# Feed-forward input of an encoder trunk: ten of 22 gate/up tile pairs by seven block products, low parts on VectorE, two kept operands in DRAM

## The chip, the cores and the metric

The kernel runs on one core of one Trainium2 chip. The time is that of one launch on the device in microseconds, the median of several runs. Durations come from the hardware profile of one more execution. Engines are named as the profile names them: PE is TensorE's matmul, PEld its weight load, DVE VectorE, ACT ScalarE, POOL GpSimd, SP the queue that issues every DMA here. L and a number is a line of the kernel before; lines of the changed kernel are said to be its.

## What is computed

Two layers; each is a feed-forward, a token mixer, and a feed-forward, with a layer norm behind each. The change touches only the four feed-forwards (x is 512 x 1024, w_in 1024 x 5632, w_out 2816 x 1024, all float32):

```python
def swiglu(x, w_in, w_out):
    gate, up = jnp.split(x @ w_in, 2, axis=-1)
    return (jax.nn.silu(gate) * up) @ w_out
...
x = layer_norm(DN_ALPHA * x + 0.5 * swiglu(x, ffn_w_in[i, 0], ffn_w_out[i, 0]), ln_g[i, 0], ln_b[i, 0])
```

## The kernel before

Every float32 operand is held as a high part (a rounded copy, made by ScalarE) and a low part (what is left, by a subtraction): this is `split`, L276 for the high and L277 for the low part. A product is three matmuls: high by high, high by low, low by high (`mm3`, L286 to L288).

**The input half.** The hidden width of 2816 is 22 tiles of 128 channels. For each tile f the kernel loads two weight tiles of 512 KB, the gate's and the up's (`load_unit`, L245, into `raw`, two buffers; split into `w`, three buffers), and makes one projection each: 8 chunks of the 1024 input channels by 3 matmuls, 128 x 512 outputs, into a PSUM bank. A tile's two weights are called a pair below. ScalarE takes the SiLU of the gate (L491), VectorE multiplies by the up projection (L493) into `ar`.

**The output half** is a product of 2 x 2 blocks done with seven block products instead of eight. For it the loop over c (11 steps, two tiles f = 2c and 2c + 1 each, called a round below) prepares two things: `sums` loads 1 MB of w_out into `ra` (one buffer), makes four combinations (L894 to L897), writes two of them to the DRAM buffer `d_late` and splits three into `wx` (three buffers); and the rest of the loop combines `ar` (L498 to L501) and splits it: three parts into `an` (one buffer), four into `keep`, which stays in SBUF for the whole feed-forward. `early` (L923) multiplies `an` by the three `wx` for the step before; it stands behind the first tile's projections. Behind the loop four more products (V, Y, Z, Y) use the four kept parts, with weights loaded from w_out and `d_late`.

Combinations and splits of weights run on GpSimd; those of `ar` are shared between VectorE and GpSimd.

**What sets the order.** The program is written engine by engine; a scheduler orders each engine's instructions by its own timeline of the program. Each engine then works strictly in that order, and waits for what its next instruction needs. A tile's buffer is given again when the last reader of its former content is done; a load waits for that on SP.

**Where a feed-forward starts.** In all but the first, half of the first two pairs (tokens 0 to 255) is multiplied while the norm before still works; `follow` does the other half. The new `xT`, x transposed with its high and low part, is complete only then.

## Time and profile before

| | us |
|---|---|
| median of 3 runs | 2185.05 |
| lowest and highest | 2183.64, 2185.83 |
| the profiled execution | 2179.1 |
| its span | 2177.3 |
| first feed-forward, its loop | about 19 to 294 |
| granted TensorE clock, mean | 0.996 |

The span is the time from the first to the last instruction in the profile; the execution's own time is 1.8 us more. In a row of the profile's groups stand line, engine, operation, what it writes and reads, shapes, count, then busy us, mean ns of one, and idle time ahead of it with what ended it. A row that begins with two times is of a timeline: start and length. A row with three numbers between slashes gives the least, the median and the most ns of one. A row that begins with a window gives the busy us of PE, PEld, DVE, ACT and POOL with counts, the granted clock, the DMA engines' share and GB/s (or PE alone).

In the first loop a round takes 25.84 us: 114 matmuls of width 512 (96 for the two pairs, 18 for the early products), one behind the other.

### The profile page before, as it was taken

What the parts mean: (1) busy time and instruction counts of PE and PEld (TensorE: products, weight loads), DVE (VectorE), ACT (ScalarE), POOL (GpSimd) and SP (SyncE); (2) the same over time, 40 slices, a digit from 0 to 9 for tenths busy, and PEclk for the clock granted to TensorE, in tenths of its full rate; (3) what the DMA queues carried; (4) which work ended last, traced back from release to release, by engine and by line L of the source; (5) the groups of instructions that cost most, each with busy time, mean ns of one, the idle gap of its engine ahead of it and who ended that gap; (6) DMA issues with size and microseconds to landing.
All of it is one profiled execution on the core that took longest, in us unless ns stands there. A gap on an engine that the chain in (4) does not pass through costs nothing.

```text
span 2177.3 us, 35335 instructions
## 1 busy us (share of the span) xinstructions
PE 2138.7 (98%) x13952; PEld 1686.0 (77%) x13952; DVE 1052.1 (48%) x1526; ACT 954.7 (44%) x1675; POOL 1392.8 (64%) x1226
## 2 busy tenths in 40 slices
PE   9999999999999999999999999999999999999998
PEld 8888888888888888888888877446666568888876
DVE  3223355377333333553333569636888554333345
ACT  3333345377333333453333444537777434333333
POOL 5988855555478778578888543046767614877753
PEclk9999999999999999999999999999999999999999
DMA  6444462332244444544444553853444552444443
GB/s 210 150 155 144 142 230 97 116 114 76 91 162 140 141 145 136 212 141 142 144 137 144 198 175 125 288 172 104 133 122 128 165 190 83 150 135 141 140 165 126
DMA packets 145366, 321.47 MB, mean 148 GB/s; under 512 B 31056, under 2 KB 51152, under 8 KB 145200
## 3 DMA queue, kind: packets, MB, share of 16 engines
q1 hardware_dynamic: 145200, 319.21, 45.0%
q8 instruction: 110, 1.80, 0.3%
q14 instruction: 56, 0.46, 0.1%
HBM read 261.22 MB, written 45.88 MB: 141 GB/s over the span
## 4 chain that ended last, share of the span: by engine, by line
PE 91%; DMA 3%; DVE 2%; ACT 1%; issue 1%; POOL 1%; SPq 0%; DVEq 0%; ACTq 0%; POOLq 0%
PE bank L287 17%; PE bank L286 17%; PE bank L288 17%; PE bank L923 17%; PE a L1115 5%; PE bank L349 4%; PE g L1439 1%; PE y L1115 1%; DMA wv<-in_w_rv_dram 1%; PE bank L1306 1%; PE m L1115 1%; PE bank L677 1%; PE y L1614 1%; PE c L1607 1%; PE y L1637 1%
## 5 line engine op out<-in xcount | busy, mean ns | idle before, releaser
L277 POOL TENSOR_TENSOR w<-raw,w 128x1024 fp32r<-128x1024 f32 x198 | 485.7, 2455 | 224.4 <-ACT w L276 216.9
L286 PE MATMUL bank<-xT,w 128*128 128x512 f32 x1264 | 493.4, 390 | 0.0
L287 PE MATMUL bank<-xT,w 128*128 128x512 f32 x1264 | 492.3, 389 | 0.0
L288 PE MATMUL bank<-xT,w 128*128 128x512 f32 x1264 | 491.9, 389 | 0.0
L276 ACT ACTIVATE w<-raw 128x1024 fp32r<-128x1024 f32 x202 | 213.0, 1058 | 312.9 <-POOL ts L894 123.1
L493 DVE SCALAR_TENSOR_TENSOR ar<-bank,tmp 128x512 f32<-128x512 f32 x88 | 60.9, 692 | 570.3 <-PE bank L288 560.2
L288 PEld LDWEIGHTS bank<-xT,w 128*128 128x128 f32 x1264 | 237.3, 188 | 49.9
L286 PEld LDWEIGHTS bank<-xT,w 128*128 128x128 f32 x1264 | 237.3, 188 | 48.6
L287 PEld LDWEIGHTS bank<-xT,w 128*128 128x128 f32 x1264 | 237.4, 188 | 48.2
L923 PE MATMUL bank<-wx,an 128*128 128x512 f32 x792 | 187.5, 389 | 0.0
L923 PEld LDWEIGHTS bank<-wx,an 128*128 128x128 f32 x792 | 148.7, 188 | 31.2
L923 PE MATMUL bank<-w,ring 128*128 128x512 f32 x720 | 168.8, 390 | 1.9 <-POOL w L277 1.7
L277 POOL TENSOR_TENSOR wx<-ra,wx 128x512 fp32r<-128x512 f32 x132 | 167.0, 1291 | 3.1 <-ACT wx L276 3.1
L277 DVE TENSOR_TENSOR ring<-ar,ring 128x1024 fp32r<-128x1024 f32 x44 | 122.5, 2785 | 87.7 <-ACT ring L276 87.6
L923 PEld LDWEIGHTS bank<-w,ring 128*128 128x128 f32 x720 | 134.9, 188 | 31.1 <-POOL w L277 2.7
L491 ACT ACTIVATE tmp<-bank 128x512 f32<-128x512 f32 x88 | 52.6, 597 | 233.4 <-PE bank L288 233.2
L1546 POOL TENSOR_TENSOR tm<-qs,zs 128x126 f32<-128x126 f32 (+22 forms) x248 | 103.6, 418 | 79.3 <-issue 35.8
L1548 POOL TENSOR_TENSOR zs<-zs,tm 128x126 f32<-128x126 f32 (+22 forms) x248 | 110.9, 447 | 19.4
L276 ACT ACTIVATE wx<-ra 128x512 fp32r<-128x512 f32 x132 | 82.7, 632 | 79.3 <-PE bank L923 66.3
L277 POOL TENSOR_TENSOR ring<-raw,ring 128x1024 fp32r<-128x1024 f32 x24 | 60.1, 2515 | 78.8 <-ACT ring L276 78.8
L277 POOL TENSOR_TENSOR w<-xT,w 128x1024 fp32r<-128x1024 f32 x25 | 62.7, 2511 | 45.2 <-ACT w L276 45.2
L499 DVE TENSOR_TENSOR ar<-ar 128x256 f32<-128x256 f32 x44 | 90.3, 2052 | 1.5
(346 smaller groups left out, 3946.3 us busy)
## 6 DMA issues: line engine op xcount, KB each, us to landing
raw<-in_ffn_w_in_dram SPq DMA_DIRECT2D x176, 512.0 KB, 3.5
ra<-in_ffn_w_out_dram SPq DMA_DIRECT2D x44, 1024.0 KB, 4.9
xT<-d_late SPq DMA_DIRECT2D x29, 512.0 KB, 5.0
xT<-in_ffn_w_out_dram SPq DMA_DIRECT2D x23, 512.0 KB, 4.6
d_late<-ts SPq DMA_DIRECT2D x44, 256.0 KB, 3.0
d_late<-ra SPq DMA_DIRECT2D x44, 256.0 KB, 2.0
raw<-in_w_qkv_dram SPq DMA_DIRECT2D x16, 512.0 KB, 3.6
raw<-in_ffn_w_out_dram SPq DMA_DIRECT2D x12, 512.0 KB, 3.6
```

What stands on the lines that cost most here:

```text
L276: self.hi = self.nc.scalar.activation(h, raw, AF.Copy).ins
L277: self.lo = (eng or self.nc.vector).tensor_tensor(l, raw, h.bitcast(F32), ALU.subtract).ins
L286: nc.tensor.matmul(out, wh, xh, start=start, stop=False)
L287: nc.tensor.matmul(out, wh, xl, start=False, stop=False)
L288: nc.tensor.matmul(out, wl, xh, start=False, stop=stop)
L349: nc.tensor.matmul(acc[t, h], a, u[:, i, h * 512 : (h + 1) * 512], start=first and n == 0, stop=last and n == 2)
L493: nc.vector.scalar_tensor_tensor(raw[:, 3:7:3] if j else raw[:, 0:8:7], halves_of(pu), 0.5, halves_of(s), ALU.mult, ALU.mult)
L499: nc.vector.tensor_tensor(a(2), a(1), a(0), ALU.subtract)
L923: self.nc.tensor.matmul(acc, lhs, u[:, i], start=bool(first) and m == 0, stop=last and m == 2, skip_group_check=more)
L1115: self.nc.tensor.matmul(out[hs], w[:, hs], x, start=start, stop=stop)
L1546: nc.gpsimd.tensor_tensor(tv, qs[:, s, 0:s].rearrange("p (a o) -> p a o", o=1).broadcast_to([P, s, n]), zs[:, s : s + 1, c0:].broadcast_to ...
L1548: nc.gpsimd.tensor_tensor(zs[:, 0:s, c0:], zs[:, 0:s, c0:], tv, ALU.add)
```

## The change

Ten of the 22 pairs, the odd f from 3 on, are no longer computed by the plain projection. x (tokens by channels) and the pair's weights are taken as 2 x 2 blocks: input channels in two halves, tokens in two halves, gate and up as the two columns. The new class `Seven` makes seven products of blocks, each 4 chunks by 3 matmuls of 128 x 256. For it,

- `mixes` makes four combinations of the blocks of x once per feed-forward on VectorE, with splits (`right`, four ring buffers), in the two rows `gbc` and `bbc` that later hold the norm's parameters;
- `operands` loads the pair's two raw tiles and makes, in place, combinations of the weight blocks: two go to `w` (`ua`, `ub`), one to `one` and two to `pair`, single buffers in two rings;
- `products` makes the seven products in two banks. Partial results are copied from bank to bank and to `tmp` by ScalarE (the changed kernel's L971), added by VectorE (L996, L998), and gated (L1000, L1002). All pairs from f = 2 on use the same two banks.

The rings that this takes held half of `keep`: two of the four kept parts are now split into `away`, written to the DRAM buffer `d_away` each round, and read back by `recall` into freed rings for the last two products. The low parts and the combinations of `sums`, of the loop and of its weights go to VectorE; the norm's parameters are loaded behind the loop.

```diff
+SEVEN = range(3, NF, 2)
...
+        seven = Seven(self, xT, w_in)
         with self.pool("fa") as pool:
             out.pool = pool
-            keep = [self.ring().rearrange("p (i n s) -> p i n s", i=2, n=4) for _ in range(npairs)]
+            keep = [self.ring().rearrange("p (c n i s) -> p c n i s", c=2, n=2, i=2) for _ in range(npairs // 2)]
+            keep = [k[:, c] for k in keep for c in range(2)] + [seven.rest.rearrange("p (n i s) -> p n i s", n=2, i=2)]
             for c in range(npairs):
-                if c == 2 and not params:
-                    with self.behind(self.asked):
-                        params = self.ln_params(ln)
                 with self.behind(*() if c or ln else (self.asked,)):
                     out.sums(c)
                 raw = pool.tile([P, 8, 256], F32, name="ar", tag="ar", bufs=1)
                 for j in range(2):
                     f = 2 * c + j
+                    dst = raw[:, 3:7:3] if j else raw[:, 0:8:7]
                     if f == 0:
                         pps = self.follow()
+                    elif f in SEVEN:
+                        seven.products(f, dst)
                     elif not pps:
-                        us = self.units if f == 1 else [self.load_cols(w_in, FF * i + f * P) for i in range(2)]
-                        pps = [self.proj_cols(u, xT) for u in us]
-                    pg, pu = pps.pop(0), pps.pop(0)
-                    s = self.tmp()
-                    nc.scalar.activation(s, pg, AF.Silu)
-
-                    nc.vector.scalar_tensor_tensor(raw[:, 3:7:3] if j else raw[:, 0:8:7], halves_of(pu), 0.5, halves_of(s),
-                                                   ALU.mult, ALU.mult)
+                        us = self.units if f == 1 else [self.load_cols(w_in, FF * i + f * P, eng=nc.vector) for i in range(2)]
+                        pps = [self.proj(u, pp, xT) for u, pp in zip(us, seven.banks(f))]
+                    if pps:
+                        pg, pu = pps.pop(0), pps.pop(0)
+                        s = self.tmp()
+                        nc.scalar.activation(s, pg, AF.Silu)
+
+                        nc.vector.scalar_tensor_tensor(dst, halves_of(pu), 0.5, halves_of(s), ALU.mult, ALU.mult)
+                    if f < 2:
+                        seven.mixes(f)
                     if j == 0 and c:
                         out.early(c - 1)
                 a = lambda n: raw[:, n]
                 nc.vector.tensor_tensor(a(1), a(7), a(6), ALU.add)
                 nc.vector.tensor_tensor(a(2), a(1), a(0), ALU.subtract)
-                nc.gpsimd.tensor_tensor(a(4), a(0), a(7), ALU.subtract)
-                nc.gpsimd.tensor_tensor(a(5), a(3), a(2), ALU.subtract)
+                nc.vector.tensor_tensor(a(4), a(0), a(7), ALU.subtract)
+                nc.vector.tensor_tensor(a(5), a(3), a(2), ALU.subtract)
                 out.now[c] = pool.tile([P, 2, 3, 256], F32R, name="an", tag="an", bufs=1)
                 self.split(out.now[c][:, 0], out.now[c][:, 1], raw[:, 0:3])
-                self.split(keep[c][:, 0], keep[c][:, 1], raw[:, 3:7])
-            out.keep = keep
+                self.split(keep[c][:, :, 0], keep[c][:, :, 1], raw[:, 3:5])
+                tag = ("gbc", "bbc")[c % 2]
+                away = self.home(self.sb).tile([P, 2, 2, 256], F32R, name="away", tag=tag)
+                self.split(away[:, :, 0], away[:, :, 1], raw[:, 5:7])
+                nc.sync.dma_start(self.away[:, :, c], away.bitcast(F32).rearrange("p n i s -> p n (i s)"))
...
+            out.recall(2)
...
+            out.recall(3)
...
+class Seven:
+    def __init__(self, k, xT, w_in):
+        self.k, self.nc, self.xT, self.w = k, k.nc, xT, w_in
+        self.own = None
+        self.right = [k.ring().rearrange("p (i c s) -> p i c s", i=2, c=4) for _ in range(4)]
+        self.pair = k.ring().rearrange("p (i f) -> p i f", i=2)
+        ring = k.ring()
+        self.one, self.rest = ring[:, :D].rearrange("p (i f) -> p i f", i=2), ring[:, D:]
+    def banks(self, f):
+        if f < 2:
+            return [self.k.bank() for _ in range(2)]
+        if self.own is None:
+            self.own = [self.k.bank() for _ in range(2)]
+        return self.own
+    def block(self, q, h):
+        return self.xT.s[q][:, :, h]
+    def mixes(self, part):
+        nc, k = self.nc, self.k
+        sub, add = ALU.subtract, ALU.add
+        tt = nc.vector.tensor_tensor
+        part_of = lambda b, i: b[:, i].bitcast(F32)
+        x, y = (k.home(k.sb).tile([P, D], F32, name="mixed", tag=t).rearrange("p (c s) -> p c s", c=4) for t in ("gbc", "bbc"))
+        def difference(out, t, a, b):
+            tt(out, part_of(a, 0), part_of(b, 0), sub)
+            tt(t, part_of(a, 1), part_of(b, 1), sub)
+            tt(out, out, t, add)
+        def fold(out, a, t):
+            tt(out, part_of(a, 0), t, sub)
+            tt(out, out, part_of(a, 1), add)
+        def keep(n, t):
+            k.split(self.right[n][:, 0], self.right[n][:, 1], t)
+        if part:
+            difference(x, y, self.block(1, 1), self.block(0, 1))
+            keep(2, x)
+        else:
+            difference(x, y, self.block(0, 1), self.block(0, 0))
+            keep(0, x)
+            fold(y, self.block(1, 1), x)
+            keep(1, y)
+            fold(x, self.block(1, 0), y)
+            keep(3, x)
+    def operands(self, f):
+        k, nc = self.k, self.nc
+        tt = nc.vector.tensor_tensor
+        raws = [k.raw() for _ in range(2)]
+        for i, raw in enumerate(raws):
+            k.asked = nc.sync.dma_start(raw, self.w[NF * i + f]).ins
+        (g0, g1), (u0, u1) = ((raw[:, :512], raw[:, 512:]) for raw in raws)
+        units = [k.sb_w.tile([P, 2 * D], F32R, name="w", tag="w", bufs=k.nw).rearrange("p (i f) -> p i f", i=2) for _ in range(2)]
+        k.split(units[0][:, 0], units[0][:, 1], raws[0])
+        tt(g0, g0, u0, ALU.subtract)
+        tt(u0, u0, u1, ALU.add)
+        k.split(units[1][:, 0], units[1][:, 1], raws[1])
+        tt(u0, u1, g0, ALU.subtract)
+        tt(g1, g1, u0, ALU.subtract)
+        k.split(self.one[:, 0], self.one[:, 1], u0)
+        k.split(self.pair[:, 0], self.pair[:, 1], raws[0])
+        return units
+    def products(self, f, dst):
+        k, nc = self.k, self.nc
+        ua, ub = self.operands(f)
+        lo, hi = slice(0, 512), slice(512, 1024)
+        a, e = self.banks(f)
+        a, f, e = a[:, :256], a[:, 256:], e[:, :256]
+        s, v, p = k.tmp(), k.tmp(), k.tmp()[:, :256]
+        s, v = halves_of(s), halves_of(v)
+        copy = lambda out, x: nc.scalar.activation(out, x, AF.Copy)
+        first = []
+        def mul(out, w, x, start):
+            for c in range(4):
+                cs = slice(c * P, c * P + P)
+                for n, (i, j) in enumerate(((0, 0), (0, 1), (1, 0))):
+                    m = nc.tensor.matmul(out, w[:, i, cs], x[:, j, c], start=start and c + n == 0, stop=c == 3 and n == 2,
+                                         skip_group_check=True)
+                    if c + n == 0:
+                        first.append(m.ins)
+        b, t = self.block, self.right
+        mul(a, ua[:, :, lo], b(0, 0), True)
+        copy(e, a)
+        with k.behind(first[0]):
+            mul(f, ub[:, :, lo], t[0], False)
+        copy(p, f)
+        mul(e, self.one, t[1], False)
+        copy(v[:, 0], e)
+        mul(a, ua[:, :, hi], b(1, 0), False)
+        nc.scalar.activation(s[:, 0], a, AF.Silu)
+        mul(e, self.pair[:, :, lo], t[2], False)
+        copy(v[:, 1], e)
+        nc.vector.tensor_tensor(v[:, 1], v[:, 1], p, ALU.add)
+        mul(f, self.pair[:, :, hi], b(1, 1), False)
+        nc.vector.tensor_tensor(v[:, 0], f, v[:, 0], ALU.add)
+        nc.scalar.activation(s[:, 1], v[:, 0], AF.Silu)
+        nc.vector.scalar_tensor_tensor(dst[:, 1], v[:, 1], 0.5, s[:, 1], ALU.mult, ALU.mult)
+        mul(e, ub[:, :, hi], t[3], False)
+        nc.vector.scalar_tensor_tensor(dst[:, 0], e, 0.5, s[:, 0], ALU.mult, ALU.mult)
...
-        nc.gpsimd.tensor_tensor(t3, r[:, 1, 1], r[:, 0, 1], ALU.subtract)
-        nc.gpsimd.tensor_tensor(r[:, 0, 1], r[:, 0, 1], r[:, 0, 0], ALU.subtract)
-        nc.gpsimd.tensor_tensor(r[:, 1, 1], r[:, 1, 1], r[:, 0, 1], ALU.subtract)
-        nc.gpsimd.tensor_tensor(r[:, 1, 0], r[:, 1, 0], r[:, 1, 1], ALU.subtract)
+        nc.vector.tensor_tensor(t3, r[:, 1, 1], r[:, 0, 1], ALU.subtract)
+        nc.vector.tensor_tensor(r[:, 0, 1], r[:, 0, 1], r[:, 0, 0], ALU.subtract)
+        nc.vector.tensor_tensor(r[:, 1, 1], r[:, 1, 1], r[:, 0, 1], ALU.subtract)
+        nc.vector.tensor_tensor(r[:, 1, 0], r[:, 1, 0], r[:, 1, 1], ALU.subtract)
         nc.sync.dma_start(self.late[:, 0, c], t3)
         nc.sync.dma_start(self.late[:, 1, c], r[:, 1, 0])
         self.units[c] = []
         for raw in (r[:, 0, 0], r[:, 1, 1], r[:, 0, 1]):
             u = self.pool.tile([P, 2, 512], F32R, name="wx", tag="wx", bufs=3)
-            k.split(u[:, 0], u[:, 1], raw, nc.gpsimd)
+            k.split(u[:, 0], u[:, 1], raw)
...
+    def recall(self, n):
+
+        rings = [self.k.ring().rearrange("p (c f) -> p c f", c=4) for _ in range(3)]
+        self.keep[n] = []
+        for i, r in enumerate(rings):
+            m = min(4, NF // 2 - 4 * i)
+            self.nc.sync.dma_start(r[:, :m].bitcast(F32), self.k.away[:, n - 2, 4 * i : 4 * i + m])
+            self.keep[n] += [r[:, c].rearrange("p (i s) -> p i s", i=2) for c in range(m)]
```

Three places of the engines' orders. A name's number tells buffers' contents apart.

**VectorE in the round c = 4** of the first feed-forward, before. From the gated product of the even tile (L493) to that of the next round; all of the weights' low parts are on GpSimd:

```order
L493 SCALAR_TENSOR_TENSOR ar_945<-bank_981,tmp_1006 128x2x256
L493 SCALAR_TENSOR_TENSOR ar_945<-bank_1062,tmp_1087 128x2x256
L498 TENSOR_TENSOR ar_945<-ar_945 128x256
L499 TENSOR_TENSOR ar_945<-ar_945 128x256
L277 TENSOR_TENSOR an_1094<-ar_945,an_1094 128x768
L277 TENSOR_TENSOR ring_262<-ar_945,ring_262 128x1024
L493 SCALAR_TENSOR_TENSOR ar_1117<-bank_1153,tmp_1178 128x2x256
```

The changed kernel, from the same gated product (now L496) to the sum L998 that reads the odd pair's bank. `raw_1212` and `raw_1213` are the odd pair's raw tiles, `ring_260` is `pair`, `raw_1359` and `raw_1364` the next even pair's, `ra_1114` and `ra_1340` the single `ra` buffer's content for this and the next `sums`:

```order
L496 SCALAR_TENSOR_TENSOR ar_1132<-bank_458,tmp_1191 128x2x256
L278 TENSOR_TENSOR ring_260<-raw_1212,ring_260 128x1024
L504 TENSOR_TENSOR ar_1132<-ar_1132 128x256
L278 TENSOR_TENSOR wx_1123<-ra_1114,wx_1123 128x512
L278 TENSOR_TENSOR wx_1126<-ra_1114,wx_1126 128x512
L278 TENSOR_TENSOR w_1360<-raw_1359,w_1360 128x1024
L278 TENSOR_TENSOR wx_1129<-ra_1114,wx_1129 128x512
L1020 TENSOR_TENSOR ts_1342<-ra_1340 128x512
L278 TENSOR_TENSOR w_1365<-raw_1364,w_1365 128x1024
L996 TENSOR_TENSOR tmp_1231<-tmp_1231,tmp_1232 128x256
L1021 TENSOR_TENSOR ra_1340<-ra_1340 128x512
L998 TENSOR_TENSOR tmp_1231<-bank_457,tmp_1231 128x256
```

VectorE had seven operations in more than a round; now twelve lie between two results that TensorE works for. `ring_260` stands behind L496, L1020 directly behind the last reader of `ra_1114`, and L998 behind L1020. In the odd rounds (c = 3, 5, 7, 9) the low part of `one` and L504 stand between L496 and `pair`'s, the three `wx` rows ahead of the gate's `w`, and L1020 to L1022 ahead of the up unit's.

**ScalarE in the same round**, before, from the even tile's SiLU to the odd tile's:

```order
L491 ACTIVATE tmp_1006<-bank_956 128x512
L276 ACTIVATE w_1033<-raw_1032 128x1024
L276 ACTIVATE ring_261<-ar_773 128x1024
L276 ACTIVATE w_1119<-raw_1118 128x1024
L276 ACTIVATE wx_936<-ra_927 128x512
L276 ACTIVATE wx_939<-ra_927 128x512
L276 ACTIVATE wx_942<-ra_927 128x512
L491 ACTIVATE tmp_1087<-bank_1037 128x512
```

The changed kernel, from the split of `one` on; `bank_458<-bank_457` is the copy of P1's result on which the third product adds:

```order
L277 ACTIVATE ring_261<-raw_1213 128x512
L277 ACTIVATE ring_260<-raw_1212 128x1024
L277 ACTIVATE wx_1123<-ra_1114 128x512
L277 ACTIVATE wx_1126<-ra_1114 128x512
L277 ACTIVATE w_1360<-raw_1359 128x1024
L277 ACTIVATE wx_1129<-ra_1114 128x512
L971 ACTIVATE bank_458<-bank_457 128x256
L971 ACTIVATE tmp_1232<-bank_457 128x256
L971 ACTIVATE tmp_1231<-bank_458 128x256
L993 ACTIVATE tmp_1230<-bank_457 128x256
```

ScalarE had loads and splits alone there; now the split of the next gate's raw tile, `w_1360<-raw_1359`, stands ahead of copies that TensorE's products wait for.

**VectorE at the start of the second feed-forward**, before: the last two blocks of the transposed x, then the gated products.

```order
L277 TENSOR_TENSOR xT_4464<-bank_4638,xT_4464 128x4x128
L277 TENSOR_TENSOR xT_4465<-bank_4639,xT_4465 128x4x128
L277 TENSOR_TENSOR xT_4464<-bank_4640,xT_4464 128x4x128
L277 TENSOR_TENSOR xT_4465<-bank_4641,xT_4465 128x4x128
L493 SCALAR_TENSOR_TENSOR ar_4980<-bank_4770,tmp_5077 128x2x256
L493 SCALAR_TENSOR_TENSOR ar_4980<-bank_4772,tmp_5080 128x2x256
L498 TENSOR_TENSOR ar_4980<-ar_4980 128x256
```

The changed kernel, from the first combination of x (L921) on:

```order
L921 TENSOR_TENSOR mixed_5657<-xT_5045 128x1024
L278 TENSOR_TENSOR xT_5046<-bank_5222,xT_5046 128x4x128
L922 TENSOR_TENSOR mixed_5658<-xT_5045 128x1024
L278 TENSOR_TENSOR wx_5548<-ra_5539,wx_5548 128x512
L278 TENSOR_TENSOR wx_5551<-ra_5539,wx_5551 128x512
L278 TENSOR_TENSOR wx_5554<-ra_5539,wx_5554 128x512
L278 TENSOR_TENSOR w_5715<-raw_5714,w_5715 128x1024
L923 TENSOR_TENSOR mixed_5657<-mixed_5657,mixed_5658 128x1024
L278 TENSOR_TENSOR w_5720<-raw_5719,w_5720 128x1024
L496 SCALAR_TENSOR_TENSOR ar_5557<-bank_5351,tmp_5654 128x2x256
L926 TENSOR_TENSOR mixed_5658<-xT_5046,mixed_5657 128x1024
L278 TENSOR_TENSOR ring_5525<-mixed_5657,ring_5525 128x1024
```

Behind the last blocks of x VectorE had next to nothing; now `mixes`, the low parts of weights and the sums stand there, 42 operations from L921 to the low part of `one` of the first seven-product pair.

## Prediction

> **What bounds the kernel now.** I read the page's busy table and slices first, then its chain, then a window inside the first feed-forward loop.

> ```profile
> span 2177.3 us, 35335 instructions
> PE 2138.7 (98%) x13952; PEld 1686.0 (77%) x13952; DVE 1052.1 (48%) x1526; ACT 954.7 (44%) x1675; POOL 1392.8 (64%) x1226
> PE 91%; DMA 3%; DVE 2%; ACT 1%; issue 1%; POOL 1%; SPq 0%; DVEq 0%; ACTq 0%; POOLq 0%
> 110.00:280.00 170.00, 170.00 (x751) 140.76 (x750) 58.94 (x42) 58.95 (x72) 139.89 (x86) 1.00 0.43 146
> ```

> TensorE is busy 98% of the span and carries 91% of the chain. In 110 to 280 us it has no gap: 751 matmuls in 170 us, one every 0.226 us, at full clock, while GpSimd is the next busiest (82%) and VectorE works a third of the time. So here only fewer TensorE nanoseconds can pay, and anything that makes TensorE wait costs in full.

> **The matmul work.** A width of 512 costs 0.2267 us; a width of 256 is read from consecutive starts.

> ```profile
> 190.05 0.39 PE L287 MATMUL bank<-xT,w 128*128 128x512 f32 x1
> 190.27 0.39 PE L288 MATMUL bank<-xT,w 128*128 128x512 f32 x1
> ...
> 606.70 0.28 PE L287 MATMUL bank<-xT,ring 128*128 128x256 f32 x1
> 606.82 0.28 PE L288 MATMUL bank<-xT,ring 128*128 128x256 f32 x1
> 606.94 0.28 PE L286 MATMUL bank<-xT,ring 128*128 128x256 f32 x1
> ```

> Half the width costs 0.120 us, more than half the time. A pair was 2 x 24 matmuls of 512: 10.88 us. It becomes 7 x 12 of 256: 10.08 us. That is 0.80 us saved, not an eighth (1.36), and over 10 pairs in 4 feed-forwards **-32 us**. Call U the moment the plain pair's up projection ends. From U TensorE has the early output products (18 x 0.2267 = 4.08 us) and the seven products P1 to P7 (1.44 us each) before the next gate projection: ideally 14.16 us, then 10.88 us for gate and up, 25.04 us a round against 25.84 now.

> **The price of the other engines' work.**

> ```profile
> L277 DVE TENSOR_TENSOR ring<-raw,ring x3: 1218/1225/1225, 11.2 to 1367.0; 128x1024 fp32r<-128x1024 f32 x3
> L277 DVE TENSOR_TENSOR xT<-bank,xT x36: 679/684/693, 7.5 to 1827.2; 128x512 fp32r<-128x512 f32 x36
> L277 DVE TENSOR_TENSOR an<-ar,an x44: 960/1060/2168, 39.4 to 2104.0; 128x768 fp32r<-128x768 f32 x44
> L499 DVE TENSOR_TENSOR ar<-ar x44: 425/2506/2509, 37.1 to 2102.7; 128x256 f32<-128x256 f32 x44
> 11.18 2.38 DVE L277 TENSOR_TENSOR ring<-raw,ring 128x1024 fp32r<-128x1024 f32 x2
> ```

> VectorE takes 0.42, 0.68, 0.96 and 1.22 us for 256, 512, 768 and 1024 columns at best; two in a row step by about 0.07 less (2.38 for two of 1.22). L499 shows the same 256 columns at 0.43 and at 2.51 us. In the changed kernel's order GpSimd does no arithmetic in the loop behind the first plain pairs' splits, so I take the best values.

> [...]

> A round on VectorE now holds 5 operations of 1024 columns, 15 of 512, one of 768 and 8 of 256 (the 512s: seven on `ra`, four on raw, L496 and the low parts of `one`, ring and away): with steps of 1.15, 0.61, 0.89 and 0.35 about 19 us of 25. VectorE is no bound by its sum; its order decides.

> **The rounds.** The remaining rows price the chain that runs through buffers with one or two copies.

> ```profile
> raw<-in_ffn_w_in_dram SPq DMA_DIRECT2D x176, 512.0 KB, 3.5
> ra<-in_ffn_w_out_dram SPq DMA_DIRECT2D x44, 1024.0 KB, 4.9
> L276 ACT ACTIVATE w<-raw x202: 1042/1057/1082, 17.7 to 2101.5; 128x1024 fp32r<-128x1024 f32 x101
> L276 ACT ACTIVATE wx<-ra x132: 615/632/637, 22.4 to 2090.4; 128x512 fp32r<-128x512 f32 x132
> L491 ACT ACTIVATE tmp<-bank 128x512 f32<-128x512 f32 x88 | 52.6, 597 | 233.4 <-PE bank L288 233.2
> 190.77 0.69 DVE L493 SCALAR_TENSOR_TENSOR ar<-bank,tmp 128x512 f32<-128x512 f32 x1 [13.82 <-PE bank L288]
> SPq L245 <- POOL w L277: 674.4, 181, 12.4
> ```

> The last matmul above issued at 190.27, so the projection ended at 190.50, and VectorE began at 190.77: 0.26 us of hand-over. The raw tiles' DMA already waits for the split that frees its slot (SPq L245, 181 times); now that split is the last of the seven-product operands. A copy of 256 columns out of PSUM is in no row; between 0.3 and 0.6 us (half and all of L491's 0.597) I take 0.4, from the per-column step of the ScalarE rows.

> Even rounds (pairs c = 2, 4, 6, 8; the order shows c = 4). U+0.26 the gated product L496 (it stands ahead of the low part of `pair`, `ring_260`), +0.61 that low part, done U+2.1. Only then is the raw slot free: the next gate's raw lands U+5.6, ScalarE's high part ends U+6.7. **Behind it in ScalarE's queue stand `wx_1129` and the copy into `bank_458`**, done U+7.6, so P3 starts U+7.65 instead of U+6.96: TensorE waits 0.7 us. Next, VectorE's low part ends U+7.95 and the third `wx` low part U+8.6. That frees the only `ra` tile; its 1 MB lands 4.9 us later, and 0.5 more since raw_1438 is on the same queue just ahead: U+14.0. **L1020 stands there in VectorE's order and waits**; behind it the up unit's low part (1.15), L996 (0.35), L1021 (0.61) and L998 (0.42): 14.0 + 0.61 + 2.53 + 0.1 = U+17.3. L998 reads the bank that the next gate projection writes, so TensorE, done with P7 at U+14.85, waits 2.4 us more. Cost 17.3 - 14.16 = 3.1 us. The same path without the queue term gives 2.6; VectorE late by one 512 operation at U gives 3.7.

> Odd rounds (c = 3, 5, 7, 9): L496, `one`, L504, then `pair`: done U+3.05; raw U+6.55, high part U+7.65, copy U+8.05, P3 U+8.1, P7's end U+15.3. Here all three `wx` low parts come before the gate's (U+5.9), `ra` lands U+10.8, L1020 to L1022 end U+13.0, the up unit's low part 14.2, L1023, L996 and L998 15.5: gate at U+15.6. Cost 1.4 us. The last round (c = 10) has no `ra`: 0.7.

> Sum: 16 x 3.1 + 16 x 1.4 + 4 x 0.7 = **+75 us**.

> **The start of each feed-forward.** P3 of the first seven-product pair needs everything on VectorE up to `one`.

> ```profile
> 609.30 0.74 PE L286 MATMUL bank<-xT,ring 128*128 128x256 f32 x4 [0.25 <-ACT xT L276]
> 609.28 1.29 DVE L277 TENSOR_TENSOR xT<-bank,xT 128x512 fp32r<-128x512 f32 x2 [5.33 <-ACT xT L276]
> 621.45 0.69 DVE L493 SCALAR_TENSOR_TENSOR ar<-bank,tmp 128x512 f32<-128x512 f32 x1 [4.84 <-PE bank L288]
> ```

> In the second feed-forward TensorE starts its second halves at 609.30 (T) and ends them at 621.2, T+11.9; then a plain pair, the early products and P1, P2 bring it to T+29.7. VectorE starts the mixes at T+0.67, and from L921 to the low part of `one` the order has 42 operations: 18 of 1024 columns, 19 of 512, one of 768, four of 256, that is 20.7 + 11.6 + 0.9 + 1.4 = 34.6 us, so P3 cannot start before T+35.3: 5.6 us late. Twelve more operations (8.2 us) reach L998 against 7.2 us of P3 to P7: 1.0 more. In the first feed-forward a plain pair takes longer to come by, but the last GpSimd splits still hold VectorE up; I take 6.5 for all four: **+26 us** (4 x 4 if waiting time is filled better, 4 x 9 if ScalarE adds its own).

> **The other edits.** Keeping two output operands in DRAM writes 512 KB a round and reads 5.5 MB per feed-forward in stages of 15 us (66 matmuls each); their loads stand ahead of others on SP. No row shows that stage with more traffic: 0 to 3 us each, I take 1, **+4 us**, as the DMA share there is 0.52:

> ```profile
> 280.00:345.00 65.00, 64.89 (x286) 1.00 0.52 185
> ```

> `away`'s copies stand on SP before the raw load, but are done earlier in VectorE's order: nothing. The moved combinations and splits (L894 to L897, L500, L501) are in VectorE's sums.

> **The clock.** TensorE never waited long before; where it did the granted clock fell.

> ```profile
> PE a L1115 <- DMA ar<-in_rw_out_dram: 3.1, 1, 3.1
> 1709.00:1714.00 5.00, 2.17 (x24) 0.83 (x20) 0.99 (x3) 1.93 (x6) 4.14 (x12) 1.00 0.76 252
> 1714.00:1720.00 6.00, 4.02 (x23) 1.26 (x24) 0.00 (x0) 0.00 (x0) 5.06 (x13) 0.56 1.02 403
> 1720.00:1725.00 5.00, 5.00 (x48) 2.04 (x42) 2.43 (x6) 1.17 (x3) 4.22 (x11) 0.85 0.40 136
> ```

> After a wait of 3.1 us (and a shorter one just before) the mean clock of the next 6 us is 0.56. Each start has a wait of some 4 us: half clock for about 4 us costs 2, four times 8. The even rounds' 2.4 us are below that wait; I count 5 us for all sixteen (0 to 27 as below). **+13 us**.

> **Sum.** The profiled execution took 2179.1 us (span 2177.3 and 1.8 around it): -32 + 75 + 26 + 4 + 13 = +86, so 2265. The three runs' median of 2185.05 is 6 us above that execution; I put the same 6 on top: **2271 us**, 1.04 times as long.

> **Rivals.** (a) *The waits are covered* and the change pays. The place is the raw tile of the next gate: from U the copy of P3 has 6.96 us, and if the raw lands by U+4.9 instead of 5.6 (a transfer of 2.8 us instead of 3.5, or a split that is freed before L496), P3 never waits, and if `ra` then lands within 2 us, no gate does. Rounds at nothing, starts at half: -32 + 13 + 4 + 4 = -11, 2174 us. For it speaks TensorE's gapless loop under a GpSimd 82% busy; against it the tile's landing times:

> ```profile
> DMA to landing us min/median/max: 3.3/3.5/8.5
> ```

> The shortest of all raw transfers took 3.3. With the full starts it is -32 + 26 + 4 + 8 = +6, 2191, near no change. (b) *Only the copy waits*: if `ra` lands before VectorE needs it, even rounds cost 0.7 and odd 1.1: 16 x 0.7 + 16 x 1.1 + 4 x 0.7 = 32 in place of 75, and the clock 8: +38, 2223. Against it: L1020 stands right behind the split that frees `ra`. (c) *The clock falls in every even round*: half clock for 3.4 us, 1.7 lost sixteen times, +27 in place of 5: +108, 2293, and 2303 with starts at 9.

> [...]

> **Chances.** Forecast 0.50, (b) 0.20, (c) 0.15, (a) 0.08 with its gain and 0.07 with full starts; of those last 0.04 fall within 0.2% (about what a measurement of this kernel can tell from no change), 0.03 above. So faster 0.08, same 0.04, slower 0.88. The forecast alone reaches from 2245 (even rounds at 2.6, starts at 4, clock 5) to 2299 (even rounds at 3.7, odd 1.9, starts at 9). To hold 8 in 10 the range takes in (b), with 18 below it for shorter waits, and (c), with transfers that land 1 us later in every round (36 more): 2205 to 2340, leaving out (a).

> **What would show it.** Right: P3 (L979) idle about 0.7 and 1.1 us behind ScalarE's copy L971, and in even rounds a second wait of about 2.4 us of the gate projection behind VectorE, with VectorE itself idle at L1020 until `ra` lands; even rounds 28.2 us, odd ones 26.4 us long; one wait of 4 to 6 us at the first P3 of each feed-forward. The matmuls' step of 0.120 us stays. Wrong: no idle TensorE in a window of rounds (rival a), or L1020 found ready (b), or a clock under 0.9 over whole loops (c). The weakest steps are the landing times, taken from a queue with less traffic.

## The result, and the profile after

| | us |
|---|---|
| before, median of 4 runs | 2185.44 |
| after, median of 4 runs (2289.64 to 2302.0) | 2293.91 |
| after over before, 95% interval | 1.0502, 1.0467 to 1.0537 |
| profiled execution after, its span | 2302.0, 2300.1 |
| granted TensorE clock, mean, before and after | 0.996 and 0.978 |

The change makes the kernel 5% slower; 4% was forecast. The profiled execution is the slowest of the four, so its sums run some 8 us above the median.

The page of the changed kernel: span, busy time of the engines, the chain by engine, and two DMA issues (KB of one, median us to landing).

```profile
span 2300.1 us, 39118 instructions
...
PE 2147.4 (93%) x15392; PEld 1749.3 (76%) x15392; DVE 1581.6 (69%) x2542; ACT 1101.9 (48%) x2015; POOL 521.1 (23%) x670
...
PE 64%; DVE 15%; DMA 14%; ACT 3%; issue 3%; SPq 0%; DVEq 0%; ACTq 0%
...
raw<-in_ffn_w_in_dram SPq DMA_DIRECT2D x176, 512.0 KB, 4.2
ra<-in_ffn_w_out_dram SPq DMA_DIRECT2D x44, 1024.0 KB, 6.0
```

TensorE's share of the chain fell from 91% to 64%; VectorE and DMA took it over, and the transfers got slower (raw from 3.5, `ra` from 4.9). The same window of the first loop as in the prediction (PE, PEld, DVE, ACT, POOL busy, clock, DMA share, GB/s):

```profile
110.00:280.00 170.00, 158.04 (x915) 138.95 (x914) 117.89 (x178) 73.69 (x116) 0.00 (x0) 0.99 0.45 149
```

Where it had no gap, TensorE now idles for 12 of 170 us. What it waited for (us in all, times, longest), then VectorE's largest wait:

```profile
PE bank L979 <- ACT bank L971: 66.6, 40, 11.3
PE bank L287 <- DVE tmp L998: 45.2, 31, 3.3
```

```profile
DVE ts L1020 <- DMA ra<-in_ffn_w_out_dram: 182.6, 36, 8.1
```

These are the two waits that were forecast, ScalarE's copy and VectorE held at L1020 ahead of L998. Now one even round, c = 2, from U = 82.58, on TensorE, ScalarE, VectorE and SP:

```profile
86.66 1.59 PE L979 MATMUL bank<-xT,w 128*128 128x256 f32 x12
88.88 1.69 PE L979 MATMUL bank<-ring,w 128*128 128x256 f32 x12 [0.63 <-ACT bank L971]
...
100.14 0.79 PE L287 MATMUL bank<-xT,w 128*128 128x512 f32 x1 [2.38 <-DVE tmp L998]
```

```profile
86.98 1.06 ACT L277 ACTIVATE w<-raw 128x1024 fp32r<-128x1024 f32 x1 [0.85 <-DMA raw<-in_ffn_w_in_dram]
87.95 0.61 ACT L277 ACTIVATE wx<-ra 128x512 fp32r<-128x512 f32 x1
88.47 0.36 ACT L971 ACTIVATE bank<-bank 128x256 f32<-128x256 f32 x1
```

```profile
96.99 0.69 DVE L1020 TENSOR_TENSOR ts<-ra 128x512 f32<-128x512 f32 x1 [7.09 <-DMA ra<-in_ffn_w_out_dram]
```

```profile
83.08 2.06 SPq L246 DMA_DIRECT2D raw<-in_ffn_w_in_dram  x2
```

L1020 started at U+14.4 (forecast 14.0) and the gate at U+17.6 (forecast 17.3). But the product that waits 0.63 us for the copy reads `ring,w`: it is the **second** one (`ub` by the first combination of x), not the third, which reads rings alone. It follows right behind P1, whose sum the copy reads. It writes the other half of the bank that the copy reads (`f` and `a` in the code).

Finally the start of the second feed-forward, on the same four engines:

```profile
662.20 1.59 PE L979 MATMUL bank<-xT,w 128*128 128x256 f32 x12
679.15 2.93 PE L979 MATMUL bank<-ring,w 128*128 128x256 f32 x12 [11.26 <-ACT bank L971]
```

```profile
677.77 1.06 ACT L277 ACTIVATE w<-raw 128x1024 fp32r<-128x1024 f32 x1 [3.56 <-DMA raw<-in_ffn_w_in_dram]
678.73 0.37 ACT L971 ACTIVATE bank<-bank 128x256 f32<-128x256 f32 x1
```

```profile
673.48 1.82 DVE L278 TENSOR_TENSOR ring<-raw,ring 128x512 fp32r<-128x512 f32 x2
...
676.20 0.69 DVE L1020 TENSOR_TENSOR ts<-ra 128x512 f32<-128x512 f32 x1 [0.30 <-DMA ra<-in_ffn_w_out_dram]
676.81 0.68 DVE L496 SCALAR_TENSOR_TENSOR ar<-bank,tmp 128x512 f32<-128x512 f32 x1
```

```profile
674.20 1.46 SPq L246 DMA_DIRECT2D raw<-in_ffn_w_in_dram  x2
```

VectorE ends `one`'s low part at 674.16, 34.7 us behind T (639.42 here), as forecast. But the matmul started only at 679.15: that low part frees the raw slot, the next gate's raw lands 3.6 us later, its high part takes 1.06, and the copy stands behind it.

The loss by term, for the profiled executions. A loss is the step between the starts of two consecutive matmuls less 0.2267 or 0.120 us, summed over the four feed-forwards, and put to what TensorE waited for; steps at half clock are a row of their own.

| term | forecast | measured |
|---|---|---|
| the matmuls themselves | -32 | -31.4 |
| rounds: copy (36 times) and gate (31 times) | +75 | 30.3 + 50.1 = +80.4 |
| four starts | +26 | +42.7 |
| late products | +4 | 0 |
| half clock | +13 | +20.9 |
| other steps | | +2.4 |
| outside the feed-forwards | 0 | +7.8 |
| sum | +86 | +122.8 |

The 7.8 lie in the second token mixer, whose code the change leaves alone. It took 518 us in the profile before and 527 in the profile after; in the eleven experiments' profiles it took 519 to 527.

### The profile page after: what moved, and what is told of

It is laid out like the page before. It is cut to its first block, busy times and chain, and to the rows that moved or that the text cites. A ratio compares the mean times of both kernels' runs of the same rounds, so it can differ in the third digit from the quotient of the medians.

```text
span 2300.1 us, 39118 instructions
## 1 busy us (share of the span) xinstructions
PE 2147.4 (93%) x15392; PEld 1749.3 (76%) x15392; DVE 1581.6 (69%) x2542; ACT 1101.9 (48%) x2015; POOL 521.1 (23%) x670
## 4 chain that ended last, share of the span: by engine, by line
PE 64%; DVE 15%; DMA 14%; ACT 3%; issue 3%; SPq 0%; DVEq 0%; ACTq 0%
PE bank L1058 15%; DMA ra<-in_ffn_w_out_dram 8%; PE bank L287 8%; PE bank L288 7%; PE bank L289 7%; PE a L1250 5%; PE bank L979 4%; PE bank L350 4%; DVE w L278 3%; DMA raw<-in_ffn_w_in_dram 3%; DVE wx L278 1%; DVE ring L278 1%; ACT w L277 1%; PE g L1574 1%; PE y L1250 1%
## 5 line engine op out<-in xcount | busy, mean ns | idle before, releaser
L278 POOL TENSOR_TENSOR w<-raw,w 128x1024 fp32r<-128x1024 f32 x38 | 93.4, 2463 | 1301.0 <-ACT w L277 1295.4
L287 PE MATMUL bank<-xT,w 128*128 128x512 f32 x704 | 285.1, 405 | 45.3 <-DVE tmp L998 45.2
L277 ACT ACTIVATE w<-raw 128x1024 fp32r<-128x1024 f32 x202 | 212.6, 1056 | 154.1 <-PE bank L979 82.3
L288 PE MATMUL bank<-xT,w 128*128 128x512 f32 x704 | 279.8, 397 | 0.0
L289 PE MATMUL bank<-xT,w 128*128 128x512 f32 x704 | 278.3, 396 | 0.0
L278 DVE TENSOR_TENSOR w<-raw,w 128x1024 fp32r<-128x1024 f32 x164 | 200.2, 1221 | 75.1 <-ACT w L277 75.1
L979 PE MATMUL bank<-ring,w 128*128 128x256 f32 x960 | 136.6, 293 | 66.6 <-ACT bank L971 66.6
L287 PEld LDWEIGHTS bank<-xT,w 128*128 128x128 f32 x704 | 134.9, 192 | 78.6 <-DVE tmp L998 51.8
L979 PEld LDWEIGHTS bank<-ring,w 128*128 128x128 f32 x960 | 124.4, 197 | 75.6 <-ACT bank L971 75.6
L289 PEld LDWEIGHTS bank<-xT,w 128*128 128x128 f32 x704 | 135.4, 192 | 29.6
L1020 DVE TENSOR_TENSOR ts<-ra 128x512 f32<-128x512 f32 x44 | 30.4, 690 | 182.6 <-DMA ra<-in_ffn_w_out_dram 182.6
L288 PEld LDWEIGHTS bank<-xT,w 128*128 128x128 f32 x704 | 135.6, 193 | 26.4
L277 ACT ACTIVATE ring<-raw 128x512 fp32r<-128x512 f32 (+1 forms) x107 | 95.8, 900 | 101.8 <-DVE raw L956 71.8
L979 PE MATMUL bank<-ring 128*128 128x256 f32 x960 | 130.7, 286 | 0.0
L979 PEld LDWEIGHTS bank<-ring 128*128 128x128 f32 x960 | 123.5, 196 | 0.1
L277 ACT ACTIVATE wx<-ra 128x512 fp32r<-128x512 f32 x132 | 81.5, 629 | 81.8 <-PE bank L1058 78.0
L278 DVE TENSOR_TENSOR wx<-ra,wx 128x512 fp32r<-128x512 f32 x132 | 96.9, 741 | 34.6 <-ACT wx L277 34.6
## 6 DMA issues: line engine op xcount, KB each, us to landing
raw<-in_ffn_w_in_dram SPq DMA_DIRECT2D x176, 512.0 KB, 4.2
ra<-in_ffn_w_out_dram SPq DMA_DIRECT2D x44, 1024.0 KB, 6.0
d_away<-away SPq DMA_DIRECT2D x44, 512.0 KB, 3.0
ring<-d_away SPq DMA_DIRECT2D x16, 1024.0 KB, 11.7
xT<-d_late SPq DMA_DIRECT2D x29, 512.0 KB, 8.5
xT<-in_ffn_w_out_dram SPq DMA_DIRECT2D x23, 512.0 KB, 8.2
```

What stands on the lines that cost most here:

```text
L277: self.hi = self.nc.scalar.activation(h, raw, AF.Copy).ins
L278: self.lo = (eng or self.nc.vector).tensor_tensor(l, raw, h.bitcast(F32), ALU.subtract).ins
L287: nc.tensor.matmul(out, wh, xh, start=start, stop=False)
L288: nc.tensor.matmul(out, wh, xl, start=False, stop=False)
L289: nc.tensor.matmul(out, wl, xh, start=False, stop=stop)
L979: m = nc.tensor.matmul(out, w[:, i, cs], x[:, j, c], start=start and c + n == 0, stop=c == 3 and n == 2, skip_group_check=True)
```

## The experiments

Every ratio is to the kernel before, run on the same chip; line numbers shift by up to four, since edits add lines. Gains in us are differences of these medians; the kernel before had 2183 to 2186 us on each of the chips used.

| | us | ratio, 95% interval |
|---|---|---|
| e1 high parts behind the copy | 2248.92 | 1.0290, 1.0271 to 1.0309 |
| e2 sums of `ra` behind L998 | 2249.50 | 1.0285, 1.0269 to 1.0302 |
| e3 both | 2232.42 | 1.0212, 1.0196 to 1.0227 |
| e4 no seven-product pair | 2184.70 | 1.0002, 0.9986 to 1.0017 |
| e5 first one at f = 5 | 2253.87 | 1.0318, 1.0292 to 1.0344 |
| e6 early products between P1 and P2 | 2239.69 | 1.0236, 1.0204 to 1.0268 |
| e7 e3 with e6 | 2223.35 | 1.0174, 1.0147 to 1.0201 |
| e8 e7 with e5 | 2192.75 | 1.0044, 1.0025 to 1.0064 |
| e9 e8, high parts behind the third copy | 2178.68 | 0.9973, 0.9960 to 0.9986 |
| e10 e9, combinations of x a tile later | 2171.10 | 0.9937, 0.9925 to 0.9949 |
| e11 e3 with the copy made twice | 2247.66 | 1.0297, 1.0274 to 1.0321 |

**e1: the plain pairs' high parts behind the copy.** An order on ScalarE's queue alone:

```diff
-        copy(e, a)
+        self.copied = [copy(e, a).ins]
...
-                        us = self.units if f == 1 else [...]
+                        with self.behind(*seven.copied):
+                            us = self.units if f == 1 else [...]
```

> Base: the changed kernel, 2294 us, where TensorE waits 66.6 us for the copy L971 (42.0 of it at the four starts, 11.3 us each in three of them) and 45.2 us for L998. Here ScalarE's high parts of the plain pairs' weights are put behind the copy. Theory 1 (the copy waits only since the next gate's high part, and with it a raw transfer, stands ahead of it; in the rounds ra decides when the gate starts): the starts fall to about 6 us each (VectorE's 34.7 us up to the low part of `one` remain), -20 us and 2 to 4 us of clock; the 24.6 us of the rounds' P3 waits go, but the gate's waits take most of it back (45 becomes 60 to 70). Together 2265 to 2272. Theory 2 (VectorE alone sets the starts, and the queue order on ScalarE matters nothing): the starts stay at 11 us, 2285 to 2295.

It gained 45 us, more than either theory gave, and not where theory 1 put it. TensorE's waits, then the second feed-forward's start on VectorE and ScalarE:

```profile
PE bank L980 <- ACT bank L972: 58.7, 40, 10.6
PE bank L287 <- DVE tmp L999: 15.0, 29, 1.5
```

```profile
661.95 0.69 DVE L1021 TENSOR_TENSOR ts<-ra 128x512 f32<-128x512 f32 x1 [0.35 <-DMA ra<-in_ffn_w_out_dram]
662.56 0.68 DVE L497 SCALAR_TENSOR_TENSOR ar<-bank,tmp 128x512 f32<-128x512 f32 x1
```

```profile
663.27 0.37 ACT L972 ACTIVATE bank<-bank 128x256 f32<-128x256 f32 x1 [3.37 <-DVE ar L497]
```

The starts stayed at 8 to 11 us: a second chain nearly as long lies under the first. The copy writes into the bank that the plain pair's gated product (L497 here) reads, and this stands on VectorE behind `one`, `pair`, `away` and L1021. The gate's waits fell from 45 to 15 us instead of rising. The scheduler answered the edit: in the even rounds `ra`'s third low part now stands ahead of the gate's on VectorE, so the next `ra` is issued at a median of U+5.7 instead of U+6.8, and their gates came at a mean of U+15.4 instead of U+16.4. That this order alone brought the gain was not tested.

**e2: the sums of `ra` behind L998.**

```diff
-        nc.vector.tensor_tensor(t3, r[:, 1, 1], r[:, 0, 1], ALU.subtract)
+        with k.behind(*after):
+            nc.vector.tensor_tensor(t3, r[:, 1, 1], r[:, 0, 1], ALU.subtract)
```

(`after` holds L998 of the round before.)

> The four combinations of `sums` are put behind L998 on VectorE; nothing else is changed. Theory 1 (the gate waits since L998 stands behind L1020, which waits for ra): VectorE's wait at L1020 (182.6 us) falls to under 30, the gate's waits fall from 45 to under 10 us and the half clock in the rounds (about 14 us) goes with them; the P3 waits stay at about 66. 2235 to 2250. Theory 2 (ra's transfer is late for whoever waits, and the early products or wx would wait in its place): a new wait of TensorE for wx or an, and under 10 us gained: 2284 to 2295. Theory 3 (VectorE is full, the order matters little): the gate's waits stay above 30 us with VectorE busy, 2270 to 2290.

Theory 1 held, to the time:

```profile
PE bank L979 <- ACT bank L971: 72.3, 40, 9.2
PE a L1251 <- DVE yt L1833: 7.7, 3, 2.6
PE bank L1059 <- DVE w L278: 5.3, 4, 1.4
```

The gate's wait is gone from the list, and the copy's stayed. So the gate waited for VectorE's place in line, not for the transfer of `ra`.

**e3: both edits together.**

> Both edits. Theory 1: the rounds lose nearly all waits (under 15 us in all), the starts 6 us each, the half clock nearly gone in the feed-forwards: 2294 - 20 (starts) - 25 (P3 in the rounds) - 37 (gates) - 20 (clock) = 2192, between 2185 and 2205. Each edit alone gives less than its share, since one wait hides in the other. Theory 3 (VectorE is full): rounds above 26 us with VectorE over 90% busy, 2230 or more.

It missed by 40 us. One round (TensorE, ScalarE) shows what is left:

```profile
112.71 1.59 PE L980 MATMUL bank<-xT,w 128*128 128x256 f32 x12
114.76 1.70 PE L980 MATMUL bank<-ring,w 128*128 128x256 f32 x12 [0.46 <-ACT bank L972]
```

```profile
114.34 0.37 ACT L972 ACTIVATE bank<-bank 128x256 f32<-128x256 f32 x1 [0.80 <-PE bank L980]
114.62 1.05 ACT L277 ACTIVATE w<-raw 128x1024 fp32r<-128x1024 f32 x1
```

Nothing stands ahead of the copy now, ScalarE itself waits for TensorE, and TensorE still idles 0.46 us ahead of the second product. From P1's last start to P2's first it is 0.74 us instead of 0.12. The 0.62 us come with every pair, 40 x 0.62 = 25 us of the 32 that the products save. The changed kernel had it already: in 17 of its 36 rounds the wait for the copy is this 0.46 us and no more. The starts still lose 36.

**e11: the copy made twice, on top of e3.**

```diff
+        copy(e, a)
         self.copied = [copy(e, a).ins]
```

> The version with both edits of order (2232 us; one wait of 0.46 us in nearly every round) with the copy of P1's sum into bank_458 made twice. Theory A (the second product stands for the copy, since it writes the bank that the copy reads, whatever else happens): each of these waits grows by the step of a second copy, 0.26 to 0.37 us, so the 36 of the rounds go from 0.46 to about 0.75 and the time by 10 to 15 us: 2242 to 2247. Theory B (the second product waits for something that ends at the same time, and the copy lies beside it): the wait stays at 0.46 and the time within 5 us of 2232.

```profile
115.33 1.69 PE L980 MATMUL bank<-ring,w 128*128 128x256 f32 x12 [0.86 <-ACT bank L972]
```

```profile
114.51 0.77 ACT L972 ACTIVATE bank<-bank 128x256 f32<-128x256 f32 x2 [0.80 <-PE bank L980]
```

The two copies take 0.77 us instead of 0.37, and in nearly every round the wait went from 0.46 to 0.86 us, the time up by 15 us (40 x 0.40 = 16), a little over theory A's 10 to 15 since its step of 0.26 to 0.37 was short. The second product waits for the copy: the wait grew by the 0.40 us that the copying took longer.

**e6 and e7: the 18 early products between P1 and P2**, on the changed kernel (e6) and on e3 (e7):

```diff
-                    if j == 0 and c:
+                    if j == 0 and c and f + 1 not in SEVEN:
                         out.early(c - 1)
...
         copy(e, a)
+        early()
```

> The changed kernel with the 18 early products moved in between the first and the second of the seven products. Theory A (the second product writes the other half of the bank that the copy L971 reads, and stands for that copy in every pair: 0.62 us from the last start of P1 to the first of P2 above the 0.12 of a step, in each of 40 pairs; with 4.08 us of other products between, it is hidden): TensorE no longer waits for L971 in the rounds (24.6 us gone), but in the changed kernel ra sets the gate in most rounds and takes more than half of it back, and the starts stay: 2272 to 2290. Theory B (the wait is ScalarE's queue alone): the same place keeps waits of about 0.4 us or more in each round.

> The same on top of both edits of order (2232 us, a round of 25.77 us with one wait, 0.46 us, behind L971). Theory A: that wait goes and with it 0.62 us a round, 25.1 us a round; starts stay at 9 us: 2232 - 22 to 25 = 2205 to 2212. Theory B (ScalarE's queue; or the wait goes over to a later product or the next gate): 25.5 us a round or more, 2222 or more.

In both the copy's wait remains at the four starts alone: for e6

```profile
PE bank L979 <- ACT bank L971: 42.1, 4, 11.4
...
PE bank L979 <- ACT tmp L971: 8.4, 5, 2.8
```

so the mechanism of theory A holds; its times do not. e6 gained 54 us where 4 to 22 were expected: from the round c = 3 on, its VectorE order has L1020 (there L1021) behind L998 (there L999), so it holds the edit of e2 too. (Its profiled execution took 2223.5 us, 16 less than the median.) e7 gained 9 on e3 instead of 20 to 27. Of the 22 us gained in its rounds, 16 came back as waits for the later copies into `tmp`:

```profile
PE bank L980 <- ACT bank L972: 35.8, 4, 9.2
PE bank L980 <- ACT tmp L972: 16.4, 17, 2.4
```

**e4: no seven-product pair**, `SEVEN = ()`, combinations of x left out, everything else of the change kept.

> No pair by seven products and no combinations of x (left out: mixes); the rest of the change stays (low parts and sums on VectorE, two kept operands by way of DRAM). Theory 1 (the loss is in the two chains that the seven products wait for, the rest costs nothing but the recall): no waits in the loops, 25.84 us a round, 2183 to 2192. Theory 2 (traffic to and from DRAM or the low parts on VectorE cost a good part): TensorE waits in the loop or in the four late products, 2200 or more.

```profile
110.00:280.00 170.00, 170.00 (x751) 140.77 (x751) 96.44 (x135) 60.38 (x79) 0.00 (x0) 1.00 0.49 166
```

The same 751 matmuls in 170 us as before. Moving all low parts to VectorE and two operands through DRAM costs nothing by itself (0.9986 to 1.0017 of the time before). The loss comes only together with the seven products and the combinations of x, which e4 leaves out as well; that the moved work is harmless beside them does not follow, since L1020, which holds the gate in the changed kernel, is part of it.

**e5: the first such pair at f = 5**, `SEVEN = range(5, NF, 2)`.

> The changed kernel with its first seven-product pair at f = 5 instead of 3 (nine pairs a feed-forward, f = 3 is a plain one). Theory 1 (the starts are VectorE's 34.7 us from the first combination of x to `one`, and behind them a raw transfer, its high part and the copy; one more plain round covers both): the four waits of 8 to 11 us (42.0 in all) and their half clock (about 8) go, the rounds keep theirs, four pairs lose 0.2 to 0.8 us each: 2240 to 2250. Theory 2 (the backlog only moves on to the next round): waits of over 4 us at f = 5, 2265 or more.

```profile
PE bank L979 <- ACT bank L971: 44.8, 33, 2.8
PE bank L287 <- DVE tmp L998: 18.4, 15, 2.4
```

The longest wait for the copy is 2.8 us instead of 11.3: the starts' 42 us are gone, as theory 1 had it: one more plain pair covers VectorE's backlog. The time fell by 40 us, a little less than theory 1's 44 to 54; in the rounds the copy's waits grew (from 24.6 to 44.8 us) and the gate's fell (from 45.2 to 18.4).

**e8, e9, e10: a version that pays.** e8 puts e3, e5 and e6 together.

> All of it: both edits of order, the early products between, first seven-product pair at f = 5. Theory 1 with A: 2208 - 4 x 9.2 (starts) - 8 (clock) + 3 (four pairs fewer) = 2166, between 2158 and 2178, faster than before by about 1%. If any of the four terms is wrong, 2185 or more.

It gave 2192.75 instead of 2166. Its largest wait in the feed-forwards, then a round of the fourth one (TensorE, ScalarE), tell why:

```profile
PE bank L980 <- ACT tmp L972: 15.2, 10, 3.6
```

```profile
1970.29 1.60 PE L980 MATMUL bank<-ring 128*128 128x256 f32 x12
1973.33 1.68 PE L980 MATMUL bank<-held,w 128*128 128x256 f32 x12 [1.45 <-ACT tmp L972]
```

```profile
1971.43 1.06 ACT L277 ACTIVATE w<-raw 128x1024 fp32r<-128x1024 f32 x1 [2.46 <-DMA raw<-in_ffn_w_in_dram]
1972.39 0.61 ACT L277 ACTIVATE wx<-ra 128x512 fp32r<-128x512 f32 x1
1972.91 0.64 ACT L972 ACTIVATE tmp<-bank 128x256 f32<-128x256 f32 x2
```

The first copy is safe, but the second and third now stand behind the same high part, which waits for its raw transfer; the fourth product writes the bank that the second of them reads (`a` and `f` again). e9 moves the high parts behind the third copy:

```diff
-        self.copied = [copy(e, a).ins]
+        copy(e, a)
...
-        copy(v[:, 0], e)
+        self.copied = [copy(v[:, 0], e).ins]
...
-            out.add("V", 0, out.b21, range(0, late))
+            with self.behind(*seven.copied):
+                out.add("V", 0, out.b21, range(0, late))
```

> The version of 2192.75 us, in which the high parts of the plain weights now stand behind the third of L971's copies (the one after the third product) instead of the first, those of the first weights of the late product too. Theory 1 (of the 35 us that the feed-forwards still lose in it, 16 are the fourth product's, which waits since the copies of the second and third stand behind a high part whose raw transfer is late): these 16 go and 3 to 5 of half clock: 2170 to 2178, 0.992 to 0.996 of before. Theory 2 (the high part itself is then late and the next gate waits for it): 2185 to 2195.

e10 puts the combinations of x behind f = 1 and f = 2:

```diff
-                    if f < 2:
-                        seven.mixes(f)
+                    if 0 < f < 3:
+                        seven.mixes(f - 1)
```

> The same with the combinations of x put one tile later (behind the gated products of f = 1 and f = 2). Theory 1 (the 7.8 us of waits of the plain gates for L496 in the first rounds come from the combinations that stand ahead of it on VectorE): 4 to 8 us less than the version with the third copy, 2164 to 2174. Theory 2 (they are needed as early as that, or the gate waits for other work of VectorE): the same time or more, with a wait at the first seven-product pair.

e9 gained 14 us, just short of the 15 to 23 of theory 1, and the fourth product's waits went from 15.2 us to 2.7:

```profile
PE bank L981 <- ACT tmp L973: 2.7, 4, 1.1
```

e10 gained 8 more. With the whole computation in it, it is 0.63% faster than before:

```profile
110.00:280.00 170.00, 170.00 (x1006) 151.67 (x1005) 132.06 (x201) 83.85 (x128) 0.00 (x0) 1.00 0.52 173
```

In this window TensorE has no gap again. Nine pairs a feed-forward should save 36 x 0.80 = 29 us; 14 come out, since 9 us of waits for the late product's first weights and some small ones remain.

## Why the prediction came out as it did

**The sign and both waits were right, and the size was near.** The loss was 108 us between the medians and 123 between the profiled executions, for 86. The matmul saving was 31.4 us for 32. L1020 held VectorE for `ra`, and with its place in line changed (e2) the gate's wait vanished. The rival in which `ra` lands early did not come, and neither did the covered waits.

**The step on the copy was wrong, and its sum came out by luck** (30.3 us for the 32 of the copy alone). I gave the copy until U+6.96, where the third product starts, and counted 25.04 us a round as the ideal. It has no slack at all: P2 directly behind P1 writes the copied bank. e3 shows it left with nothing else in the way, e11 doubles it, e6 hides it. So 25.66 us is the round without any queueing, and with TensorE's products in this order even perfect timing of the other engines could keep only 7 of the 32 us. In e3 the copy ran until 114.71 and P2 started at 114.76, in e11 the two copies until 115.28 and P2 at 115.33, although P2 writes the half of the bank that they do not read. No run lets the second product start while the copy reads, so what would come of that is not shown.

**The raw slot** of the next gate is freed by `one`'s low part, not by `pair`'s. In the round shown its load went out at U+0.5, not U+2.1, and the copy was late by less than I had. Over 16 even rounds the gate came at a mean of U+16.4, not 17.3; over 16 odd rounds at U+16.9, not 15.6. That 75 came so near to 80.4 is luck too: these errors nearly cancelled.

**The starts were mis-sized**, 26 for 42.7. `one`'s low part came at T+34.7 (forecast T+35.3). I ended the chain there, although the chain that I had priced in the rounds, raw slot, transfer, high part, copy, hangs on that very low part: 5 us more. And e1 showed a second chain through the gated product L496, only some 1 us shorter (10.1 for 11.3 us of waiting in the second feed-forward).

**The clock** cost 20.9 us for 13. The starts cost the 8 that I had. I counted 5 us for sixteen rounds, as 2.4 us of waiting, less than the 3.1 of the one wait that I had, seemed too short to halve it; eight gate waits of 1.8 to 3.3 us were followed by half clock and cost 12 us. The 3.4 us of half clock in rival (c) stand in no row of the prediction; the profile before has one such stretch (0.50 from 1605.47 to 1608.89), and each of the eight was followed by one of 3.41 us.

**VectorE's best values** held: the four 256-column combinations (L502 to L505 there) took 0.41 to 0.43 us each, 44 times, with GpSimd at 0.00 us in the window of 110 to 280. That GpSimd's work is what made L499 slow before was my estimate; no run tests it alone.

**The late products** cost nothing in the changed kernel for the 4 that I had; the recall's traffic is covered there.

## What to carry to other kernels

When a product is split so that partial sums are copied between matmuls, count each copy in series where the next product writes the bank that the copy reads: here 0.62 us each ate three quarters of the gain, and with 4.08 us of other products between (e6) the copy's wait was left at the four starts alone. When pricing a wait, follow the chain to the matmul itself, through whatever stands ahead on each queue, and then look for the next longest chain, since removing one wait here twice uncovered another. A small change of order on one in-order queue can be worth more than the arithmetic that it serves: e2, four operations put behind another on VectorE, gained 44 us where the products save 32. e10, with several such changes, has the changed kernel's products, but for one pair a feed-forward, and is 123 us faster.

## What the runs showed of the hardware

```profile
208.00:213.00 5.00, 2.70 (x15) 2.19 (x14) 5.00 (x8) 2.02 (x3) 0.00 (x0) 1.00 0.48 157
213.00:218.00 5.00, 5.00 (x23) 4.13 (x23) 3.94 (x9) 1.14 (x2) 0.00 (x0) 1.00 0.13 52
...
295.00:298.00 3.00, 1.18 (x8) 0.85 (x7) 3.00 (x6) 1.90 (x3) 0.00 (x0) 1.00 0.41 61
298.00:301.50 3.50, 3.50 (x10) 2.73 (x9) 2.79 (x6) 0.12 (x1) 0.00 (x0) 0.51 0.47 172
```

The first wait, 2.30 us (5.00 less 2.70), lay across two cells, with 0.51 us of idle time in one and 1.80 in the next, and left the clock at 1.00; the second, 1.82 us, lay within one and was followed by 0.51.
